# The index keys' projection of a two-layer trunk with x held in the array and 80 weight columns moving past it

## The chip, the cores and the metric

The kernel runs on one core of a Trainium2 chip, as one program. The metric is the device time in microseconds (us), the median of several runs. The profile is that of one execution of its own, whose time is given beside its span.

## What is computed

Two residual layers over 256 tokens of 2048 features, batch 1, all in float32. Layer 0 is a stick-breaking attention and an MLP; layer 1 is an indexer-selected sparse attention and an MLP (2048 to 8192, squared ReLU, back to 2048). The change lies in layer 1, in the indexer. Cut to what matters:

```python
h = rms_norm(x, norm_mix[1])
q, k, v, qi, ki, wi = split(h @ w_in_b)       # 2048, 512, 512, 1024, 64, 16 columns
qi = qi.reshape(b, s, 16, 64)
wi = wi * 16 ** -0.5
for each block of 128 queries:
    dots = einsum('bqhd,bkd->bqhk', qi_block, ki) * 64 ** -0.5
    score = einsum('bqh,bqhk->bqk', wi_block, relu(dots))
    sel = top_k(score where admissible, 64)
    ... softmax attention over the selected keys ...
```

`ki` is one index key of 64 features for each token, and `wi` one weight for each token and index head. Together they are 80 columns of `w_in_b`, and they are all that the change touches.

## The kernel before, in words

**Items.** All the dense work is one list of 738 items. An item is a block of weights, 128 partitions by 1024 numbers (two blocks of 128 rows by 512 columns). For each item the program loads the block from HBM by the SP queue (`load`, L815), splits it into a rounded part `wh` (a copy on ScalarE, L84) and the rest `wl` (a subtraction on VectorE, L839), and multiplies. Three matmuls stand for one product: x-high by w-high, x-high by w-low, x-low by w-high, all in the type fp32r. An ordinary item thus has 12 matmuls of 128 rows by 128 columns held in the array and 512 columns moving (L281 to L283). In these the activations `xT` (features on the partitions, tokens on the free side) are held and the weights move. Item i's multiplication stands in the program behind the split of item i+2 and the load of item i+7: five raw buffers, three split ones.

**The items of the indexer.** In the section of mixer B (`mixer_b`, L521), items 0 to 15 make the queries of the index heads (`qi`), items 16 and 17 the 80 columns of `ki` and `wi` (`ki_part`, L551), items 18 to 25 the attention's keys, and then queries, values and the output projection follow. `k0` is 18. The two items of `ki_part` are smaller blocks: 8 blocks of rows by 80 columns. They are the only dense items in which the weights are held (80 columns) and x moves: 16 matmuls with 512 columns moving, x-high and x-low side by side (L558), and 16 with 256 columns (L559).

**What follows the sums.** `ki_done` (L563) takes the sums, features first, out of PSUM: a copy on ScalarE (`kc`), an addition on VectorE (`ku`), a multiplication by `RS` into `kiT` (64 partitions), and a DMA on the ScalarE queue that copies it to partitions 64 to 127. `RS` holds each token's RMS scale along the free side; `row_scale_wide` (L231) makes it with two transposes on TensorE (L234) and a copy. `wi_step` (L574), two items later, turns the 16 columns of `wi` back to tokens first by two transposes on TensorE (L578).

**Turning by DRAM.** Other parts are turned by `to_features` (L156): VectorE transposes blocks of 32 by 32, four DMAs on the SP queue write the result to DRAM so many items later, and one DMA reads it back, turned, four items after that (`later`, L152, hangs a step on the end of an item).

**Order.** The scheduler may move an instruction within its engine; those passed through `keep` stand behind everything that the program gave that engine before. The steps of the indexer hang on items by hand (L783 to L789): `wi_step` at `k0+1`; eight score steps (L585, matmuls of 64 rows, a ReLU on ScalarE, four VectorE operations) at `k0+6` to `k0+12`; the causal limit at `k0+13`; top-k at `k0+14` to `k0+17`; the mask at `k0+18`. `acc` has three PSUM buffers of two banks, `aux` two of one bank, and the tile `jx`, which `to_features` fills, three buffers.

Of the kernel before, what the change touches and what calls it, by code (L numbers as in the profile page):

```python
# [9 lines left out]
F32 = mybir.dt.float32  # L10
# [7 lines left out]
P = 128  # L18
D = 2048
S = 256  # L20
KT = D // P
# [37 lines left out]
def trunk(ctx, tc, x, x_t, gains_t, w_in_a, w_out_a, w_in_b, w_out_b, rel_bias, w_up, w_down, out):  # L59


    nc = tc.nc
    x, out = x[0], out[0]
    w_in_a, w_out_a, w_in_b, w_out_b = w_in_a[0], w_out_a[0], w_in_b[0], w_out_b[0]

    consts = ctx.enter_context(tc.tile_pool(name="consts", bufs=1))
    wpool = ctx.enter_context(tc.tile_pool(name="wpool", bufs=3))
    tmp = ctx.enter_context(tc.tile_pool(name="tmp", bufs=2))
    accp = ctx.enter_context(tc.tile_pool(name="accp", bufs=3, space=PSUM))
    auxp = ctx.enter_context(tc.tile_pool(name="auxp", bufs=2, space=PSUM))  # L70
    drp = ctx.enter_context(tc.tile_pool(name="drp", bufs=1, space=bass.MemoryType.DRAM))

    act, dve, pool, pe = nc.scalar, nc.vector, nc.gpsimd, nc.tensor
# [5 lines left out]
    def pin(ins):  # L79
        if pinned[0]:  # L80
            keep(ins)

    def copy(o, i, scale=1.0):
        pin(act.activation(o, i, AF.Copy, scale=scale))  # L84
# [20 lines left out]
    ident = consts.tile([P, P], F32, name="ident")  # L105
# [19 lines left out]
    xT = consts.tile([P, KT, 2, S], F32R, name="xT")  # L125
    ss = consts.tile([P, 2, 4], F32, name="ss")
    rs = consts.tile([P, 2], F32, name="rs")
    consts.tile([P, 98], F32, name="pad2")
    RS = consts.tile([P, S], F32, name="RS")

    def load_x(lo, hi):
        pin(nc.sync.dma_start(xs[:, :, lo:hi], x[:, lo:hi].rearrange("(t p) d -> p t d", p=P)))
# [19 lines left out]
    def later(n, f, *a):  # L152

        due[clock[0] + n].append(lambda: f(*a))

    def to_features(parts, place, then, wait=0):  # L156


        n = sum(part.shape[1] // P for part in parts)
        y = tmp.tile([P, 8, P], F32, name="jx", bufs=3)[:, :n, :]  # L160
        m = 0
        for part in parts:
            k = part.shape[1] // P
            dve.transpose(y[:, m:m + k, :].rearrange("p k f -> p (k f)"), part)  # L164
            m += k
        d = drp.tile([4, 32, n, 4, 32], F32, name=f"td{n}", bufs=4)

        def write():
            for a in range(4):
                keep(nc.sync.dma_start(d[:, :, :, a, :].rearrange("b j n i -> j n b i"),  # L170
                                       y[32 * a:32 * a + 32].rearrange("p n (b i) -> p n b i", b=4)))
            later(4, read)

        def read():
            z = place()
            keep(nc.sync.dma_start(z, d.rearrange("b j n a i -> (b j) n (a i)")))
            if then is not None:
                later(4, then, z)

        later(1 + wait, write)  # L180
# [33 lines left out]
    def rsqrt(o, m, n):  # L214

        y = tmp.tile([P, 8], F32, name="rs_y")
        z = tmp.tile([P, 8], F32, name="rs_z")
        act.activation(y[:, :n], m, AF.Ln)
        act.activation(y[:, :n], y[:, :n], AF.Exp, scale=-0.5)
        dve.tensor_mul(z[:, :n], y[:, :n], y[:, :n])  # L220
        dve.tensor_mul(z[:, :n], z[:, :n], m)
        dve.tensor_scalar(z[:, :n], z[:, :n], -0.5, 1.5, op0=OP.mult, op1=OP.add)
        dve.tensor_mul(o, y[:, :n], z[:, :n])

    def row_scale():
        m = tmp.tile([P, 2], F32, name="rs_m")
        dve.tensor_reduce(m, ss, axis=AX.X, op=OP.add)
        dve.tensor_scalar(m, m, 1.0 / D, EPS, op0=OP.mult, op1=OP.add)
        rsqrt(rs, m, 2)

    def row_scale_wide():  # L231
        ps = auxp.tile([P, 512], F32, name="aux")
        for t in range(2):
            pe.transpose(ps[:, t * P:(t + 1) * P], rs[:, t:t + 1].to_broadcast([P, P]), ident)  # L234
        dve.tensor_copy(RS, ps[:, :S])


    accs = {}
# [1 line left out]
    def rows(w, r0, nr, c0, ncol):  # L240
        return w[r0:r0 + nr, c0:c0 + ncol].rearrange("(a p) c -> p a c", p=P)
# [279 lines left out]
    def mixer_b():  # L521
        items = []
        st = {}
# [17 lines left out]

        TOKS = (slice(0, P), slice(P, 384))

        def stats():
            row_scale()
            row_scale_wide()

        def qi_done(s, acc):
            to_features(acc, lambda: st["qiT"][:, s], None)

        def ki_part(q):  # L551
            def mm(wh, wl):
                if q == 0:
                    accs["ki"] = accp.tile([P, 2, 512], F32, name="acc")
                acc = accs["ki"]
                for j in range(8):
                    k = 8 * q + j
                    pe.matmul(acc[:80, 0, :], wh[:, j, :], xT[:, k, :, :], start=(k == 0), stop=False)  # L558
                    pe.matmul(acc[:80, 0, 0:S], wl[:, j, :], xT[:, k, 0, :], start=False,  # L559
                              stop=(k == KT - 1))  # L560
            return Item(rows(w_in_b, 8 * P * q, 8 * P, 4096, 80), 8, 80, mm)

        def ki_done():  # L563
            acc = accs.pop("ki")
            c = tmp.tile([P, S], F32, name="kc", bufs=1)
            u = tmp.tile([P, S], F32, name="ku", bufs=1)
            copy(c[:80, :], acc[:80, 0, S:])
            dve.tensor_add(u[:80, :], acc[:80, 0, :S], c[:80, :])
            kiT = st["kiT"]
            dve.tensor_mul(kiT[0:64, :], u[0:64, :], RS[0:64, :])  # L570
            nc.scalar.dma_start(kiT[64:128, :], kiT[0:64, :])
            st["u"] = u

        def wi_step():  # L574
            u = st.pop("u")
            ps = auxp.tile([P, 512], F32, name="aux")
            for t in range(2):
                pe.transpose(ps[:, t * P:t * P + 80], u[:80, t * P:(t + 1) * P], ident[:80, :80])  # L578
            r32 = tmp.tile([P, 2], F32, name="r32")
            dve.tensor_scalar_mul(r32, rs, HEADS ** -0.5 * IDX_D ** -0.5)  # L580
            for t in range(2):
                dve.tensor_scalar(st["wi"][:, t, :], ps[:, t * P + 64:t * P + 80], rs[:, t:t + 1],
                                  r32[:, t:t + 1], op0=OP.mult, op1=OP.mult)

        def score_step(m):  # L585

            kiT, sc = st["kiT"], st["sc"]
            halves = [slice(0, 64), slice(64, P)]
            ps = accp.tile([P, 2, 512], F32, name="acc")
            for t, cs, w in ((0, TOKS[0], P), (1, TOKS[1], S)):  # L590
                for i, lo in enumerate(halves):
                    keep(
                        pe.matmul(ps[:, i, cs], st["qiT"][lo, m // 4, 4 * t + m % 4], kiT[lo, 0:w],  # L593
                                  start=True, stop=True))
            rl = mk([P, 2, 384], "rl")
            act.activation(rl, ps[:, :, :384], AF.Relu)
            for i in range(2):
                h, r = 2 * m + i, rl[:, i, :]
                for t, cs in enumerate(TOKS):
                    w = st["wi"][:, t, h:h + 1]  # L600
                    if h == 0:
                        dve.tensor_scalar_mul(sc[:, cs], r[:, cs], w)
                    else:
                        dve.scalar_tensor_tensor(sc[:, cs], r[:, cs], w, sc[:, cs],
                                                 op0=OP.mult, op1=OP.add)
# [61 lines left out]
        def q_done(n, acc):  # L667
            r = normed(acc)
            if n < 3:
                to_features([r[:, t].rearrange("p h d -> p (h d)") for t in range(2)],  # L670
                            lambda: q_tile(n), None, 3)
            else:
                st["qn"] = r
# [88 lines left out]
        for s, q in side_by_side(2, QB):  # L762
            tokens_out(items, ("qi", s), w_in_b, 0, 3072 + 512 * s, lambda: xT, q,
                       lambda acc, s=s: qi_done(s, acc))
        items[10].post.append(stats)
        items += [ki_part(0), ki_part(1)]
        items[-1].post.append(ki_done)
        k0 = len(items)
        for q in range(QB):
            tokens_out(items, "k", w_in_b, 0, 2048, lambda: xT, q, k_done)  # L770
        for n in (0, 1, 2, "v", 3):
            for q in range(QB):
                if n == "v":
                    tokens_out(items, "v", w_in_b, 0, 2560, lambda: xT, q, v_done)
                else:
                    tokens_out(items, ("q", n), w_in_b, 0, 512 * n, lambda: xT, q,
                               lambda acc, n=n: q_done(n, acc))
        out_proj(items, w_out_b, lambda: st["oT"], 48, 3)

        def at(i, f, *a):  # L780
            items[i].post.append(lambda: f(*a))

        at(k0 + 1, wi_step)  # L783
        for m, d in enumerate((6, 6, 8, 8, 10, 10, 12, 12)):
            at(k0 + d, score_step, m)
        at(k0 + 13, admit)
        for r in range(TOPK // 8):
            at(k0 + 14 + r // 2, top_step)
        at(k0 + 18, mask_step)  # L789
        for n, j in enumerate((34, 42, 50, 58)):  # L790
            at(j, bias_load, n)
            at(j + 4, bias_mask, n, 0)
# [7 lines left out]


    sections = [mixer_a(), mlp(0, 16), mixer_b(), mlp(1, None)]
    items = [it for sec in sections for it in sec[0]]
    first = {}
    n = 0
# [96 lines left out]
```

## Time and profile before

| | us |
|---|---|
| median of 3 runs (2084.3 to 2085.76) | 2084.66 |
| time of the profiled execution | 2085.96 |
| its span, first to last instruction | 2084.2 |
| TensorE matmul busy | 2076.0 (100%) |
| TensorE weight loads busy | 1717.6 (82%) |
| VectorE busy | 1243.1 (60%) |
| ScalarE busy | 963.4 (46%) |

The mean granted TensorE clock was 0.999 of full speed. Busy time of matmuls is a union of records that overlap: a matmul's record lasts longer than the step to the next matmul, so what one costs is read from the starts of two that follow each other, not from its length. A group row gives the line, the engine, the operation, the tiles written and read, the shape, the count, then busy us, the mean length of one in ns, and the idle time before it with what ended it. PE is TensorE's matmuls, PEld its weight loads, DVE is VectorE, ACT ScalarE, POOL GpSimd, SPq and ACTq the DMA issues of two queues. In a shape such as 128\*80, 128 rows and 80 columns are held.

### The profile page before, as it was taken

The page shows a single profiled execution, that of the slowest core. Times are in us where ns is not written, and L with a number is a line of the kernel's source. Part 1 is how long each engine was busy: PE and PEld are TensorE (multiplying, and loading weights), DVE is VectorE, ACT ScalarE, POOL GpSimd, SP SyncE. Part 2 cuts the span into 40 slices and gives each one's busy share as a digit, 9 for nine tenths or more (in the row PEclk, how much of TensorE's full clock was granted, in tenths as well). Part 3 has the DMA queues.
Part 4 walks back from the last instruction along what each step waited for, and adds up shares of the span by engine and source line. Part 5 has one row for each costly group of instructions (what it writes and reads, how often), then busy time and mean ns, then how long its engine had stood idle before and what let it go on. Part 6 is the DMA issues. An engine that isn't in the chain of part 4 may idle for free.

```text
span 2084.2 us, 24647 instructions
## 1 busy us (share of the span) xinstructions
PE 2076.0 (100%) x9256; PEld 1717.6 (82%) x9256; DVE 1243.1 (60%) x1350; ACT 963.4 (46%) x1164; POOL 25.8 (1%) x71
## 2 busy tenths in 40 slices
PE   9999999999999999999999999999999999999999
PEld 7888888888888888888888788888888888888887
DVE  5646655666655565565565898666565555555554
ACT  6545554544443443443454566554444344344433
POOL 0200000000000000000000000000000000000000
PEclk9999999999999999999999999999999999999999
DMA  8788857888866876886788698498887687688664
GB/s 294 221 239 218 238 172 200 260 243 247 231 214 196 242 223 196 233 233 192 214 254 245 183 256 255 142 274 232 258 234 213 193 235 231 194 226 244 192 203 150
DMA packets 477448, 464.83 MB, mean 223 GB/s; under 512 B 269648, under 2 KB 279952, under 8 KB 477328
## 3 DMA queue, kind: packets, MB, share of 16 engines
q1 hardware_dynamic: 469472, 455.81, 75.3%
q10 hardware_dynamic: 7856, 7.45, 1.4%
q8 instruction: 72, 1.18, 0.2%
q14 instruction: 48, 0.39, 0.1%
HBM read 425.90 MB, written 37.22 MB: 222 GB/s over the span
## 4 chain that ended last, share of the span: by engine, by line
PE 99%; DMA 0%; ACT 0%; DVE 0%; SPq 0%; issue 0%; DVEq 0%
PE acc L281 31%; PE acc L283 31%; PE acc L282 31%; PE acc L254 1%; PE aux L705 1%; PE acc L415 0%; PE aux L461 0%; DMA wraw<-in_w_in_a_dram 0%; PE acc L593 0%; PE aux L282 0%; PE aux L283 0%; PE aux L281 0%; PE acc L558 0%; PE acc L417 0%; PE aux L462 0%; PE aux L755 0%
## 5 line engine op out<-in xcount | busy, mean ns | idle before, releaser
L839 DVE TENSOR_TENSOR w<-wraw,w 128x1024 fp32r<-128x1024 f32 (+1 forms) x739 | 901.0, 1220 | 759.8 <-ACT w L84 755.6
L84 ACT ACTIVATE w<-wraw 128x1024 fp32r<-128x1024 f32 (+1 forms) x739 | 784.2, 1061 | 1037.2 <-PE acc L283 983.9
L282 PE MATMUL acc<-w,xT 128*128 128x512 f32 x1632 | 638.3, 391 | 0.0
L281 PE MATMUL acc<-w,xT 128*128 128x512 f32 x1632 | 637.4, 391 | 0.0
L283 PE MATMUL acc<-w,xT 128*128 128x512 f32 x1632 | 636.8, 390 | 0.0
L281 PE MATMUL acc<-w,hT 128*128 128x512 f32 x992 | 386.4, 389 | 0.0
L282 PE MATMUL acc<-w,hT 128*128 128x512 f32 x992 | 386.4, 389 | 0.0
L283 PE MATMUL acc<-w,hT 128*128 128x512 f32 x992 | 386.3, 389 | 0.0
L283 PEld LDWEIGHTS acc<-w,xT 128*128 128x128 f32 x1632 | 306.6, 188 | 63.9 <-issue 0.7
L281 PEld LDWEIGHTS acc<-w,xT 128*128 128x128 f32 x1632 | 306.7, 188 | 63.7 <-ACT w L84 0.3
L282 PEld LDWEIGHTS acc<-w,xT 128*128 128x128 f32 x1632 | 306.7, 188 | 63.5 <-issue 0.7
L282 PEld LDWEIGHTS acc<-w,hT 128*128 128x128 f32 x992 | 186.3, 188 | 38.6
L283 PEld LDWEIGHTS acc<-w,hT 128*128 128x128 f32 x992 | 186.3, 188 | 38.5
L281 PEld LDWEIGHTS acc<-w,hT 128*128 128x128 f32 x992 | 186.3, 188 | 38.5
L281 PE MATMUL acc<-w,oT 128*128 128x512 f32 x256 | 100.4, 394 | 0.0
L282 PE MATMUL acc<-w,oT 128*128 128x512 f32 x256 | 99.6, 390 | 0.0
L283 PE MATMUL acc<-w,oT 128*128 128x512 f32 x256 | 99.1, 391 | 0.0
L281 PEld LDWEIGHTS acc<-w,oT 128*128 128x128 f32 x256 | 48.1, 188 | 10.1 <-ACT junk L643 0.4
L283 PEld LDWEIGHTS acc<-w,oT 128*128 128x128 f32 x256 | 48.1, 188 | 9.9
L282 PEld LDWEIGHTS acc<-w,oT 128*128 128x128 f32 x256 | 48.1, 188 | 9.8
L164 DVE STREAM_TRANSPOSE jx<-acc 128x512 f32<-128x512 f32 x68 | 44.7, 695 | 14.4 <-PE acc L283 10.8
L297 DVE SCALAR_TENSOR_TENSOR xs<-acc,rs,xs 128x512 f32<-128x512 f32 x56 | 39.5, 746 | 11.2 <-PE acc L283 11.2
(149 smaller groups left out, 789.0 us busy)
## 6 DMA issues: line engine op xcount, KB each, us to landing
wraw<-in_w_up_dram SPq DMA_DIRECT2D x256, 512.0 KB, 4.1
wraw<-in_w_down_dram SPq DMA_DIRECT2D x256, 512.0 KB, 4.8
wraw<-in_w_in_a_dram SPq DMA_DIRECT2D x95, 512.0 KB, 4.8
wraw<-in_w_in_b_dram SPq DMA_DIRECT2D x64, 512.0 KB, 4.7
td<-jx SPq DMA_DIRECT2D x240, 128.0 KB, 4.5
jx<-td SPq DMA_DIRECT2D x45, 512.0 KB, 6.2
wraw<-in_w_out_a_dram SPq DMA_DIRECT2D x32, 512.0 KB, 4.0
wraw<-in_w_out_b_dram SPq DMA_DIRECT2D x32, 512.0 KB, 4.6
```

The lines of the kernel that those rows point to most:

```text
L84: pin(act.activation(o, i, AF.Copy, scale=scale))
L164: dve.transpose(y[:, m:m + k, :].rearrange("p k f -> p (k f)"), part)
L254: pin(pe.matmul(accs[key][t], L[:, j, part, t * P:(t + 1) * P], wx[:, j, :], start=(j == 0 and n == 0), stop=False))
L281: pin(pe.matmul(acc[t], L[:, k, 0, ts], wh[:, j, :], start=(k == 0), stop=False))
L282: pin(pe.matmul(acc[t], L[:, k, 0, ts], wl[:, j, :], start=False, stop=False))
L283: pin(pe.matmul(acc[t], L[:, k, 1, ts], wh[:, j, :], start=False, stop=(k == KT - 1)))
L297: dve.scalar_tensor_tensor(xc, acc[t], scale[:, t:t + 1], xc, op0=OP.mult, op1=OP.add)
L705: pe.matmul(ps[:, h - lo, :], qT[:, GRP * t + h, :], kT[:, n, 0:w], start=True, stop=True)
L839: pin(dve.tensor_sub(wl[:, a], raw[:, a], wh[:, a].bitcast(F32)))
```

## The change

The 80 columns are now what moves, and x is held, as in the ordinary items. For each half of the tokens and each of 16 blocks of features there are three matmuls with 128 by 128 of x held and 80 columns moving; the sums come out with tokens on the partitions. There each token's scale is one number for its partition, so `RS`, `row_scale_wide` and `wi_step` go: two ScalarE copies scale `ki` and write it twice side by side (`u`), and VectorE scales `wi` straight from PSUM. `ki` is then turned by `to_features`: one VectorE transpose of 256 columns, four writes to DRAM at item 18, one read at item 22 that fills all 128 partitions of `kiT`; the DMA on the ScalarE queue goes. The score steps, the causal limit, top-k and the mask hang one item later. The split parts of these two items begin 8 numbers further into their buffer, as in the ordinary items (`moving`). The tiles `RS` and `kc` (1 KB for each partition) are no longer allocated.

```diff
-    RS = consts.tile([P, S], F32, name="RS")
...
-        def stats():
-            row_scale()
-            row_scale_wide()
+        stats = row_scale
...
-                for j in range(8):
-                    k = 8 * q + j
-                    pe.matmul(acc[:80, 0, :], wh[:, j, :], xT[:, k, :, :], start=(k == 0), stop=False)
-                    pe.matmul(acc[:80, 0, 0:S], wl[:, j, :], xT[:, k, 0, :], start=False,
-                              stop=(k == KT - 1))
-            return Item(rows(w_in_b, 8 * P * q, 8 * P, 4096, 80), 8, 80, mm)
+                for t in range(2):
+                    ts = slice(t * P, (t + 1) * P)
+                    for j in range(8):
+                        k = 8 * q + j
+                        for n, (i, w) in enumerate(((0, wh), (0, wl), (1, wh))):
+                            pe.matmul(acc[:, t, :80], xT[:, k, i, ts], w[:, j, :],
+                                      start=(k, n) == (0, 0), stop=(k, n) == (KT - 1, 2))
+            return Item(rows(w_in_b, 8 * P * q, 8 * P, 4096, 80), 8, 80, mm, True)
...
-            c = tmp.tile([P, S], F32, name="kc", bufs=1)
-            u = tmp.tile([P, S], F32, name="ku", bufs=1)
-            copy(c[:80, :], acc[:80, 0, S:])
-            dve.tensor_add(u[:80, :], acc[:80, 0, :S], c[:80, :])
-            kiT = st["kiT"]
-            dve.tensor_mul(kiT[0:64, :], u[0:64, :], RS[0:64, :])
-            nc.scalar.dma_start(kiT[64:128, :], kiT[0:64, :])
-            st["u"] = u
-
-        def wi_step():
-            u = st.pop("u")
-            ps = auxp.tile([P, 512], F32, name="aux")
-            for t in range(2):
-                pe.transpose(ps[:, t * P:t * P + 80], u[:80, t * P:(t + 1) * P], ident[:80, :80])
+            u = tmp.tile([P, 2, 2, 64], F32, name="ku", bufs=1)
             r32 = tmp.tile([P, 2], F32, name="r32")
             dve.tensor_scalar_mul(r32, rs, HEADS ** -0.5 * IDX_D ** -0.5)
             for t in range(2):
-                dve.tensor_scalar(st["wi"][:, t, :], ps[:, t * P + 64:t * P + 80], rs[:, t:t + 1],
+                copy(u[:, t], acc[:, t, :64].unsqueeze(1).to_broadcast([P, 2, 64]),
+                     scale=rs[:, t:t + 1])
+                dve.tensor_scalar(st["wi"][:, t, :], acc[:, t, 64:80], rs[:, t:t + 1],
                                   r32[:, t:t + 1], op0=OP.mult, op1=OP.mult)
+            to_features([u.rearrange("p t i f -> p (t i f)")],
+                        lambda: st["kiT"].rearrange("p (t q) -> p t q", t=2), None)
...
-        at(k0 + 1, wi_step)
-        for m, d in enumerate((6, 6, 8, 8, 10, 10, 12, 12)):
+        for m, d in enumerate((7, 7, 9, 9, 11, 11, 13, 13)):
             at(k0 + d, score_step, m)
-        at(k0 + 13, admit)
+        at(k0 + 14, admit)
         for r in range(TOPK // 8):
-            at(k0 + 14 + r // 2, top_step)
-        at(k0 + 18, mask_step)
+            at(k0 + 15 + r // 2, top_step)
+        at(k0 + 19, mask_step)
```

## Rows read from the trace of the kernel before

**Rows 1.** the page, part 1 (busy us, share of the span, instructions) and the start of part 4

```profile
PE 2076.0 (100%) x9256; PEld 1717.6 (82%) x9256; DVE 1243.1 (60%) x1350; ACT 963.4 (46%) x1164; POOL 25.8 (1%) x71
...
PE 99%; DMA 0%; ACT 0%; DVE 0%; SPq 0%; issue 0%; DVEq 0%
```

**Rows 2.** the waits of TensorE: us in total, times, longest

```profile
PE acc L254 <- ACT w L84: 2.0, 2, 1.7
```

**Rows 3.** groups of TensorE by shape: count, busy us, mean ns of one, idle before

```profile
L281 PE MATMUL acc<-w,xT 128*128 128x512 f32 x1632 | 637.4, 391 | 0.0
...
L558 PE MATMUL acc<-xT,w 128*80 128x512 f32 x16 | 5.6, 395 | 0.0
...
L559 PE MATMUL acc<-xT,w 128*80 128x256 f32 x16 | 4.5, 280 | 0.0
...
L578 PE MATMUL aux<-ident,ku 80*128 80x80 f32 x2 | 0.3, 232 | 0.0
```

**Rows 4.** TensorE in order of time over the index's two items: start, length (us)

```profile
1127.39 0.39 PE L283 MATMUL acc<-w,xT 128*128 128x512 f32 x1
1127.62 0.40 PE L558 MATMUL acc<-xT,w 128*80 128x512 f32 x1
1127.86 0.28 PE L559 MATMUL acc<-xT,w 128*80 128x256 f32 x1
1127.97 0.40 PE L558 MATMUL acc<-xT,w 128*80 128x512 f32 x1
...
1133.23 0.40 PE L281 MATMUL acc<-w,xT 128*128 128x512 f32 x1
```

**Rows 5.** TensorE around the two transposes of rs

```profile
1100.17 0.39 PE L281 MATMUL acc<-w,xT 128*128 128x512 f32 x1
1100.40 0.38 PE L234 MATMUL aux<-ident,rs 128*128 128x128 f32 x2
...
1100.85 0.39 PE L283 MATMUL acc<-w,xT 128*128 128x512 f32 x1
```

**Rows 6.** TensorE around the two transposes of ku

```profile
1138.49 0.40 PE L283 MATMUL acc<-w,xT 128*128 128x512 f32 x1
1138.72 0.30 PE L578 MATMUL aux<-ident,ku 80*128 80x80 f32 x2
...
1139.14 0.39 PE L282 MATMUL acc<-w,xT 128*128 128x512 f32 x1
```

**Rows 7.** weight loads (PEld) behind the transposes of ku: start, length

```profile
1138.80 0.19 PEld L281 LDWEIGHTS acc<-w,xT 128*128 128x128 f32 x1
1138.91 0.19 PEld L282 LDWEIGHTS acc<-w,xT 128*128 128x128 f32 x1
```

**Rows 8.** weight loads behind the first two score steps

```profile
1154.14 0.19 PEld L281 LDWEIGHTS acc<-w,xT 128*128 128x128 f32 x1 [0.33 <-ACT w L84]
1154.25 0.19 PEld L282 LDWEIGHTS acc<-w,xT 128*128 128x128 f32 x1
```

**Rows 9.** ScalarE behind the index's sums: start, length, count

```profile
1133.43 0.38 ACT L84 ACTIVATE kc<-acc 80x256 f32<-80x256 f32 x1 [1.74 <-PE acc L559]
```

**Rows 10.** groups of VectorE behind the index's sums, by shape

```profile
L568 DVE TENSOR_TENSOR ku<-acc,kc 80x256 f32<-80x256 f32 x1 | 0.4, 421 | 0.9 <-ACT kc L84 0.9
L570 DVE TENSOR_TENSOR kiT<-ku,RS 64x256 f32<-64x256 f32 x1 | 0.4, 418 | 0.0
```

**Rows 11.** the SP queue: four writes of the heads' index, start, length, count

```profile
1132.31 4.48 SPq L170 DMA_DIRECT2D td<-jx  x4
```

**Rows 12.** DMA issues of 1125 to 1165 us: KB of one, median us to landing

```profile
wraw<-in_w_in_b_dram SPq DMA_DIRECT2D x13, 512.0 KB, 4.6
...
w<-td SPq DMA_DIRECT2D x2, 512.0 KB, 6.9
```

**Rows 13.** busy us of PE, PEld, DVE, ACT, POOL by stretch; clock, DMA share, GB/s

```profile
1133.00:1152.00 19.00, 19.00 (x87) 15.63 (x86) 9.57 (x11) 7.72 (x8) 0.00 (x0) 1.00 0.98 294
...
1185.00:1200.00 15.00, 15.00 (x68) 12.44 (x67) 15.00 (x51) 9.91 (x24) 0.00 (x0) 1.00 0.72 212
```

More of the change, by code (lines that the diff above doesn't have):

```diff
@@ L229, in row_scale @@
         rsqrt(rs, m, 2)
-    def row_scale_wide():
-        ps = auxp.tile([P, 512], F32, name="aux")
-        for t in range(2):
-            pe.transpose(ps[:, t * P:(t + 1) * P], rs[:, t:t + 1].to_broadcast([P, P]), ident)
-        dve.tensor_copy(RS, ps[:, :S])
     accs = {}
@@ L555, in mm @@
                 acc = accs["ki"]
-                for j in range(8):
-                    k = 8 * q + j
-                    pe.matmul(acc[:80, 0, :], wh[:, j, :], xT[:, k, :, :], start=(k == 0), stop=False)
-                    pe.matmul(acc[:80, 0, 0:S], wl[:, j, :], xT[:, k, 0, :], start=False,
-                              stop=(k == KT - 1))
-            return Item(rows(w_in_b, 8 * P * q, 8 * P, 4096, 80), 8, 80, mm)
+                for t in range(2):
[6 more added lines that the diff above has]
+            return Item(rows(w_in_b, 8 * P * q, 8 * P, 4096, 80), 8, 80, mm, True)
         def ki_done():
             acc = accs.pop("ki")
-            c = tmp.tile([P, S], F32, name="kc", bufs=1)
-            u = tmp.tile([P, S], F32, name="ku", bufs=1)
-            copy(c[:80, :], acc[:80, 0, S:])
-            dve.tensor_add(u[:80, :], acc[:80, 0, :S], c[:80, :])
-            kiT = st["kiT"]
-            dve.tensor_mul(kiT[0:64, :], u[0:64, :], RS[0:64, :])
-            nc.scalar.dma_start(kiT[64:128, :], kiT[0:64, :])
-            st["u"] = u
-        def wi_step():
-            u = st.pop("u")
-            ps = auxp.tile([P, 512], F32, name="aux")
-            for t in range(2):
-                pe.transpose(ps[:, t * P:t * P + 80], u[:80, t * P:(t + 1) * P], ident[:80, :80])
+            u = tmp.tile([P, 2, 2, 64], F32, name="ku", bufs=1)
             r32 = tmp.tile([P, 2], F32, name="r32")
```

## The prediction

> **What bounds the kernel now.** I read the page's busy times and its chain first. TensorE's matmuls are busy for 2076.0 of 2084.2 us, and the chain that ended last is TensorE for 99% [rows 1]. The waits of TensorE come next, to see whether that busy time hides stalls: the largest group is 2.0 us in two waits, at line 254, which is not in the code of this change [rows 2]. So TensorE goes from one matmul to the next almost without a gap, and what counts is the step from one start to the next. Third are the groups by shape, for the counts; their mean lengths of 391, 395 and 280 ns overlap and are no price [rows 3]. Prices come from the orders of time: an ordinary matmul with 512 columns moving steps by 0.23 us, one with 256 columns by 0.11 us [rows 4]. An item of 12 thus takes 2.7 us. The other engines work ahead of TensorE, so their work costs time only where it makes a split, a PSUM buffer or `kiT` late.
>
> **The change, part by part, on TensorE.**
>
> The old multiplication goes. Its 32 matmuls run from 1127.62 to 1133.23 us, where the next item's first matmul starts: 5.61 us [rows 4].
>
> The two transposes of `rs` go. With them, 0.68 us lie between the ordinary matmuls at 1100.17 and 1100.85, with one ordinary matmul between; two ordinary steps are 0.46 us. That gives 0.22 us [rows 5]. The two transposes of `ku` go: from 1138.49 to 1139.14 are 0.65 us against 0.46 again, so 0.19 us [rows 6]. Together 6.02 us are removed.
>
> The new multiplication has 2 halves of the tokens by 16 blocks of features by 3 matmuls: 96, against 32 before. Each holds 128 columns of x and moves 80. No row shows that shape, so it is bounded. From below, the moving columns alone: 256 take 0.11 us, so 80 in proportion would take 0.034 us, 3.3 us in all, and the change would give back 2.7 us. From above, the whole record of a weight load, 0.19 us [rows 7], with nothing overlapped: 18.2 us, a loss of 12.2 us. Between these lies what a load costs when the matmul in front of it is too short to cover it. Two places show that. Behind the short transposes of `ku` (two matmuls of 232 ns within 0.30 us, so 0.07 us apart [rows 3, 6]) the load at 1138.80 is followed by the next one at 1138.91 [rows 7]. Behind the score steps, after TensorE's loads had stood idle for 0.33 us, the loads start at 1154.14 and 1154.25 [rows 8]. Both are 0.11 us, in both the load was of 128 by 128 of `xT`, and in neither was there moving work of 0.11 us to wait for. So I take 0.11 us for each of the 96: the load sets the step, and the 80 columns run in its shadow. A held operand used twice running saves nothing: lines 281 and 282 hold the same x, and each matmul still has a load of its own, 9256 loads for 9256 matmuls [rows 1]. That makes 10.56 us. The read-off error of two decimals is a few ns a matmul: 0.105 to 0.118 us make 10.1 to 11.3 us.
>
> Sum on TensorE: 10.56 less 6.02 is **+4.5 us** (4.1 to 5.3 by that reading).
>
> **The change on the other engines.** ScalarE loses one copy of 0.38 us [rows 9] and a DMA issue and gets two copies of about that size; the next split waits behind them by some 0.4 us, and splits are made two items, 5.4 us, ahead: nothing. VectorE loses 0.42 and 0.42 us behind the sums [rows 10] and the copy to `RS`, and gets one transpose of 256 columns; it is busy for 9.57 of the 19 us there [rows 13]: nothing. If that cover were gone, either would cost at most its own length, under 0.5 us.
>
> The SP queue gets four writes and a read. The writes wait for the turn of VectorE, and behind them stand the loads of weights. Four writes of the heads' index held SP for 4.48 us [rows 11], with four times the bytes of these, so 4.48 us bounds them from above. A load is issued five items, 13.6 us, before its split and lands in 4.6 us [rows 12]: 9.0 us are spare, so nothing. The two items themselves grow by 4.5 us and need no more bytes, which helps the loads.
>
> `kiT` now comes by DRAM. Its read is due at the end of item 22 and the first score at the end of item 25: three items, 8.2 us. The two larger reads at this place took 6.9 us to land [rows 12]. I take nothing; TensorE would stand still for each us over 8.2.
>
> The score steps, the causal limit, top-k and the mask issue the same instructions one item later. Nothing is added, but VectorE has room from 1133 to 1152 us and none from 1185 to 1200, where it is busy for 15.00 of 15.00 us [rows 13]. One item's worth of room is given up ahead of a full stretch. The splits are in that same queue. The cost lies between nothing and that one item, 2.7 us; less than nothing has no cause, since no wait of TensorE at these steps is there to be saved [rows 2]. I take nothing, because TensorE had no wait in that full stretch before, and keep the end for the range. The memory that `RS` and `kc` leave moves other tiles; I take nothing, since 1632 matmuls that read three weight buffers at different places show one mean [rows 3].
>
> The profiled execution took 2085.96 us, 1.8 us over its span and 1.3 us over the median of the runs. Its own sum is 2085.96 + 4.5 = 2090.5 us; against the median 2084.66 it is **2089.2 us**, or +0.22%.
>
> **The rivals.**
>
> *Quick loads (not slower).* Place: the 96 new loads. If short matmuls let loads follow at the 0.07 us that the two `ku` transposes show [rows 6], the new multiplication takes 6.7 us and the change +0.7 us: 2085.4 us. The point from which it decides is 0.106 us a matmul, where the loss falls to 0.2%; at 0.063 us it would be nothing. For it: those two matmuls had loads as well. Against it: they are transposes, and the two loads of `xT` in a like place were 0.11 us apart [rows 7, 8]. The Trainium skill, "TensorE: Matmul & The Clock Gate", section "Back-to-back issue gap", speaks for a value between: it gives about 81 ns for a pair of weight load and matmul with 128 columns moving in a sustained stream. By that the 96 would take 7.8 us, an estimate, and the kernel 2086.4 us; the 0.11 us of the rows is not what it says. Chance 0.12.
>
> *VectorE falls behind.* The indexer's steps, one item later, run into the full stretch, a split comes late, and TensorE waits for 1 to 2.7 us between items 26 and 45: 2090.2 to 2091.9 us. For it: VectorE at 100% there [rows 13]. Against it: the scheduler can put splits ahead of top-k. Chance 0.18.
>
> *`kiT` is late.* The read through DRAM lands after 8.2 us, with DMA engines 98% busy in the stretch before [rows 13]; two us late makes 2091.2 us. Against it: a quarter of the bytes, and three items of time. Chance 0.05.
>
> *Nothing overlaps.* Load and matmul run one after the other at 0.19 us: 2096.8 us. Against it: the two pairs of loads 0.11 us apart. Chance 0.05.
>
> The forecast itself keeps 0.60.
>
> **How the numbers follow.** A difference of 0.2%, 4.2 us, is about what a measurement of this kernel can tell from no change. The forecast lies 0.3 us over it, and the runs of before spread over 1.5 us, so of its 0.60 I put 0.37 over the bound and 0.23 within. Slower: 0.37 + 0.18 + 0.05 + 0.05 = 0.65. Within: 0.23, and quick loads with most of their 0.12, 0.33. Faster, 0.02, is what is left of quick loads near the lower bound. The range takes the forecast with its reading error, the late splits and the late `kiT`: 2087.0 to 2092.0 us. It leaves out quick loads and the serial case, 0.17.
>
> **What would show it.** In the profile after, the 96 matmuls of `ki_part` start 0.11 us apart and the two items take 10.6 us where they took 5.61; steps of 0.07 or 0.04 us would prove the pricing wrong. Lines 234 and 578 are gone. TensorE's waits stay as small as in [rows 2]; a new wait of a score matmul for a DMA, or of an ordinary matmul for VectorE's split near the top-k steps, would be the second or third rival. TensorE's busy time should rise by the same 4 to 5 us as the span.

## The result and the profile after

The changed kernel takes 2099.36 us (median of 6 runs, 2098.23 to 2101.81) against 2084.61 us: 14.75 us slower, ratio 1.007 [1.0059, 1.0081]. I had forecast 2089.2 us and a range that ended at 2092.0. Its profiled execution took 2098.23 us with a span of 2096.5 us; it is the quickest of the six, so its profile shows rather less than the whole loss: the two profiled spans lie 12.3 us apart (2084.2 and 2096.5).

The page's part 1 and the start of part 4, which answer to [rows 1]:

```profile
PE 2086.8 (100%) x9316; PEld 1727.3 (82%) x9316; DVE 1241.8 (59%) x1348; ACT 963.3 (46%) x1165; POOL 25.9 (1%) x71
...
PE 96%; DVE 2%; DMA 1%; ACT 1%; issue 0%; SPq 0%; DVEq 0%; ACTq 0%
```

TensorE is still the bound, with 60 matmuls more: 64 in the index, and the four transposes gone. But the chain now has some work of VectorE, the DMAs and ScalarE in it.

Lines are numbered anew in this kernel: the ordinary matmuls, L281 to L283 before, are L274 to L276 here. The 96 new matmuls in order of time, first whole and then in two stretches, where equal neighbours are merged (start, length of the whole, count):

```profile
1125.62 15.13 PE L553 MATMUL acc<-w,xT 128*128 128x80 f32 x96
...
1126.76 2.52 PE L553 MATMUL acc<-w,xT 128*128 128x80 f32 x21
...
1132.66 5.75 PE L553 MATMUL acc<-w,xT 128*128 128x80 f32 x26
```

One record lasts 0.28 us in the first stretch and 0.41 us in the second, so the steps are (2.52 - 0.28) / 20 = 0.112 us and (5.75 - 0.41) / 25 = 0.214 us. The first is the step that the prediction had. The second is twice as long. The busy time by stretch shows why (PE, PEld, DVE, ACT, POOL busy with counts; then the granted clock, DMA share, GB/s):

```profile
1126.00:1131.00 5.00, 5.00 (x47) 5.00 (x47) 2.24 (x3) 0.88 (x1) 0.00 (x0) 1.00 1.08 207
...
1131.50:1132.00 0.50, 0.50 (x5) 0.50 (x5) 0.00 (x0) 0.50 (x1) 0.00 (x0) 0.54 0.62 102
...
1132.00:1140.00 8.00, 8.00 (x40) 8.00 (x39) 1.23 (x1) 0.16 (x1) 0.00 (x0) 0.50 0.84 189
1141.00:1145.00 4.00, 4.00 (x11) 3.03 (x11) 2.07 (x4) 1.37 (x3) 0.00 (x0) 0.50 0.13 18
1146.00:1150.00 4.00, 4.00 (x19) 3.30 (x18) 1.58 (x2) 1.91 (x2) 0.00 (x0) 1.00 0.46 95
```

The granted clock is full in the first stretch and half (1.2 of 2.4 GHz) in those of 1132 and 1141; it fell between 1131.5 and 1132, some 5.9 us into the run, though TensorE's matmuls and weight loads are recorded as busy without a gap. It is still at half when the ordinary matmuls resume:

```profile
1139.91 0.84 PE L553 MATMUL acc<-w,xT 128*128 128x80 f32 x3
1140.55 0.77 PE L274 MATMUL acc<-w,xT 128*128 128x512 f32 x1
1141.13 0.63 PE L275 MATMUL acc<-w,xT 128*128 128x512 f32 x1
...
1144.97 0.51 PE L275 MATMUL acc<-w,xT 128*128 128x512 f32 x1
1145.31 0.39 PE L276 MATMUL acc<-w,xT 128*128 128x512 f32 x1
1145.54 0.40 PE L274 MATMUL acc<-w,xT 128*128 128x512 f32 x1
```

Those with 512 columns moving step by 0.43 us, and 0.23 us again only from 1145.31. In [rows 4] the same two items took 5.61 us; here the 96 begin at 1125.62 and the next item at 1140.55, 14.9 us.

Last, the waits of TensorE inside the section, two that [rows 2] had no counterpart for (total, times, longest):

```profile
PE acc L274 <- ACT junk L629: 1.3, 1, 1.3
...
PE acc L274 <- ACT rl L582: 0.3, 1, 0.3
```

Both are ordinary matmuls that wait for a PSUM buffer `acc` until ScalarE has read it, behind the norm's squares (`junk`) and behind a score step's ReLU (`rl`).

### The profile page after: what moved, and what is told of

Same layout as the page of the kernel before. It is cut to its first block, busy times and chain, and to the rows that moved or that the text cites. A ratio compares the mean times of both kernels' runs of the same rounds, so it can differ in the third digit from the quotient of the medians.

```text
span 2096.5 us, 24767 instructions
## 1 busy us (share of the span) xinstructions
PE 2086.8 (100%) x9316; PEld 1727.3 (82%) x9316; DVE 1241.8 (59%) x1348; ACT 963.3 (46%) x1165; POOL 25.9 (1%) x71
## 4 chain that ended last, share of the span: by engine, by line
PE 96%; DVE 2%; DMA 1%; ACT 1%; issue 0%; SPq 0%; DVEq 0%; ACTq 0%
PE acc L274 30%; PE acc L275 30%; PE acc L276 30%; PE acc L247 1%; PE acc L553 1%; DVE w L824 1%; PE aux L691 0%; PE acc L408 0%; PE aux L454 0%; PE aux L276 0%; PE aux L275 0%; PE aux L274 0%; DMA wraw<-in_w_in_a_dram 0%; DMA qTb<-td 0%; ACT w L84 0%
## 5 line engine op out<-in xcount | busy, mean ns | idle before, releaser
L274 PE MATMUL acc<-w,xT 128*128 128x512 f32 x1632 | 637.6, 391 | 0.3 <-ACT rl L582 0.3
L276 PE MATMUL acc<-w,xT 128*128 128x512 f32 x1632 | 636.7, 390 | 0.0
L274 PE MATMUL acc<-w,hT 128*128 128x512 f32 x992 | 385.9, 389 | 0.0
L276 PE MATMUL acc<-w,hT 128*128 128x512 f32 x992 | 385.9, 389 | 0.0
L274 PEld LDWEIGHTS acc<-w,xT 128*128 128x128 f32 x1632 | 307.0, 188 | 64.9 <-issue 1.0
L276 PEld LDWEIGHTS acc<-w,xT 128*128 128x128 f32 x1632 | 307.0, 188 | 64.3 <-issue 0.3
L276 PEld LDWEIGHTS acc<-w,hT 128*128 128x128 f32 x992 | 186.2, 188 | 38.6
L274 PEld LDWEIGHTS acc<-w,hT 128*128 128x128 f32 x992 | 186.2, 188 | 38.6
L274 PE MATMUL acc<-w,oT 128*128 128x512 f32 x256 | 100.3, 394 | 1.3 <-ACT junk L629 1.3
L276 PE MATMUL acc<-w,oT 128*128 128x512 f32 x256 | 99.0, 391 | 0.0
L274 PEld LDWEIGHTS acc<-w,oT 128*128 128x128 f32 x256 | 48.1, 188 | 11.5 <-ACT junk L629 1.7
L276 PEld LDWEIGHTS acc<-w,oT 128*128 128x128 f32 x256 | 48.1, 188 | 9.9
L163 DVE STREAM_TRANSPOSE jx<-acc 128x512 f32<-128x512 f32 x68 | 44.7, 695 | 14.4 <-PE acc L276 10.8
```

The lines of the kernel that those rows point to most:

```text
L274: pin(pe.matmul(acc[t], L[:, k, 0, ts], wh[:, j, :], start=(k == 0), stop=False))
L276: pin(pe.matmul(acc[t], L[:, k, 1, ts], wh[:, j, :], start=False, stop=(k == KT - 1)))
```

## The experiments

Theory after this reading: the loss has three parts. Weight loads set the step (as forecast, some 5 us). The long run of matmuls that move little takes the clock to half (some 6.5 us). The later place of the score and top-k steps makes waits (some 3 us). The rival was that the steps behind the sums, with their way through DRAM, hold most of the loss, and that the clock's fall is of little weight or belongs to the place. Each group of runs had its own runs of the kernel before on the same chip: medians 2084.84 us for the first two groups, 2084.74 for the last. The changed kernel was not run again with them; its 2099.36 us is compared across, where the kernel before differs by 0.2 us.

**Four short runs in place of a long one.** The 96 matmuls are issued as four items of 24, each behind four ordinary items. (Not shown: everything behind hangs two items later in the list.)

```diff
-        items += [ki_part(0), ki_part(1)]
+            if n % 4 == 3:
+                items.append(ki_part(n // 4))
```

> The 96 matmuls are issued as four items of 24, each behind four ordinary items, in place of one run of 96; the later steps hang two items later in the list. Clock theory (the long run of matmuls with 80 columns moving takes the granted clock to half, and that costs some 6.5 us): the clock stays full, the 96 still step by 0.11 us, so about 2084.6 + 5.1 - 0.4 for the matmuls and some 2.7 for the waits behind, 2092 us (2090 to 2094). Rival (the clock's fall costs little, the loss is in the steps behind the sums): 2097 to 2100 us, as the changed kernel.

Measured: 2093.84 us, ratio 1.0043 [1.0028, 1.0058]. In order of time, one of the four:

```profile
1106.39 0.39 PE L276 MATMUL acc<-w,xT 128*128 128x512 f32 x1
1106.62 2.77 PE L553 MATMUL acc<-w,xT 128*128 128x80 f32 x24
1109.22 0.48 PE L274 MATMUL acc<-w,xT 128*128 128x512 f32 x1
```

24 take 2.60 us, the clock does not fall at any of the four, and the matmuls behind them are at full pace. So the same 96 matmuls without the long fall save 5.5 us, in a kernel that is otherwise not quite the same. It also has waits of its own further on, because all that hangs behind it moved: the keys' index comes 1.0 us late from DRAM here, and a PSUM buffer 2.0 us late.

```profile
PE acc L274 <- ACT junk L629: 2.0, 1, 2.0
...
PE acc L579 <- DMA kiT<-td: 1.0, 1, 1.0
```

Behind the wait of 2.0 us the clock did fall, for some 3 us of ordinary matmuls that step by 0.43 us:

```profile
1295.51 0.50 PE L274 MATMUL acc<-w,oT 128*128 128x512 f32 x1 [1.99 <-ACT junk L629]
...
1296.00:1299.00 3.00, 3.00 (x9) 2.33 (x8) 2.53 (x4) 2.93 (x5) 0.00 (x0) 0.50 0.08 14
```

This was the slowest of four executions, 2096.21 us; the two whose mean granted clock is given as 1.0 took 2092.00 and 2092.42 us. In this execution the wait was thus followed by a loss of clock on top of its own length.

**Fewer matmuls, wider.** x-high meets w-high and w-low in one matmul.

```diff
-                        for n, (i, w) in enumerate(((0, wh), (0, wl), (1, wh))):
-                            pe.matmul(acc[:, t, :80], xT[:, k, i, ts], w[:, j, :],
-                                      start=(k, n) == (0, 0), stop=(k, n) == (KT - 1, 2))
+                        pe.matmul(acc[:, t, :160].rearrange("p (h c) -> p h c", h=2),
+                                  xT[:, k, 0, ts], it.both[:, :, j, :], start=k == 0, stop=False)
+                        pe.matmul(acc[:, t, :80], xT[:, k, 1, ts], wh[:, j, :],
+                                  start=False, stop=k == KT - 1)
```

> x-high meets w-high and w-low in one matmul with 160 columns moving, x-low a matmul with 80: 64 matmuls in place of 96, and a copy and an addition join the two sums. If the weight load sets the step, 64 x 0.112 = 7.2 us at full clock. Clock theory does not say whether this mix keeps the clock: if it does, 2084.6 - 6.0 + 7.2 + 2.7 = 2088.5 us; if it falls some 4.4 us into the run, 2.8 us are doubled and the ordinary matmuls behind lose 2.1 us, 2093 us. If the columns set the step, the 160-column matmuls would take more than the 80-column ones.

Measured: 2088.55 us, ratio 1.0019 [1.0009, 1.0029]. In order of time, and the stretch of the 64:

```profile
1125.74 0.32 PE L552 MATMUL acc<-w,xT 128*128 128x160 f32 x1
1125.90 0.24 PE L554 MATMUL acc<-w,xT 128*128 128x80 f32 x1
1125.96 0.32 PE L552 MATMUL acc<-w,xT 128*128 128x160 f32 x1
1126.12 0.24 PE L554 MATMUL acc<-w,xT 128*128 128x80 f32 x1
```

```profile
1125.00:1132.00 7.00, 7.00 (x66) 7.00 (x64) 3.65 (x4) 2.12 (x2) 0.00 (x0) 1.00 0.94 168
```

A pair takes 0.22 us, two loads of 0.11, so a third of the loads less is a third of the time less. With this mix the clock stays full. The 4.4 us that the expectation of this run and that of the 32 matmuls give for the fall are a misreading: in the profile after it came 5.9 us into the run.

**The later place alone.** The kernel before, with only the numbers of the hanging steps changed.

```diff
-        for m, d in enumerate((6, 6, 8, 8, 10, 10, 12, 12)):
+        for m, d in enumerate((7, 7, 9, 9, 11, 11, 13, 13)):
...
-        at(k0 + 18, mask_step)
+        at(k0 + 19, mask_step)
```

> The kernel before with one part of the change alone: score steps, causal limit, top-k and mask hang one item later. If the 2.7 us that the changed kernel loses behind the index come from these later steps, 2087.3 us (2086.3 to 2088.3). If they come from the way through DRAM or the ScalarE copies, 2084.6 us within 0.5.

Measured: 2088.11 us, ratio 1.0014 [1.0004, 1.0023], 3.3 us more with no matmul changed. The two profiles, which both have a stretch at half clock in the first 20 us, differ by 2.3 us in span (2086.5 and 2084.2). Its groups of TensorE have the two waits of the changed kernel, in the idle time at the end of the rows:

```profile
L281 PE MATMUL acc<-w,xT 128*128 128x512 f32 x1632 | 636.7, 390 | 0.3 <-ACT rl L596 0.3
...
L281 PE MATMUL acc<-w,oT 128*128 128x512 f32 x256 | 100.3, 394 | 1.0 <-ACT junk L643 1.0
```

**A third of the matmuls.** One matmul for each half of the tokens and block of features in place of three; the two products with the rests are left out, so `ki` and `wi` are less exact.

```diff
-                        for n, (i, w) in enumerate(((0, wh), (0, wl), (1, wh))):
-                            pe.matmul(acc[:, t, :80], xT[:, k, i, ts], w[:, j, :],
-                                      start=(k, n) == (0, 0), stop=(k, n) == (KT - 1, 2))
+                        pe.matmul(acc[:, t, :80], xT[:, k, 0, ts], wh[:, j, :],
+                                  start=k == 0, stop=k == KT - 1)
```

> Leaves out the two cross products of ki and wi (x-high by w-low, x-low by w-high): 32 matmuls in place of 96, 3.6 us, shorter than the 4.4 us after which the clock fell. Clock theory: the clock stays full, 2084.6 - 6.0 + 3.6 + 2.7 = 2084.9 us (2083.5 to 2086). Rival (the loss is behind the sums): 2092 us or more, since only 64 matmuls of 0.11 us are saved on 2099.4.

Measured: 2085.44 us, ratio 1.0003 [0.9994, 1.0012]. The stretch of the 32 is at full clock:

```profile
1126.00:1129.50 3.50, 3.50 (x33) 3.46 (x32) 2.87 (x4) 2.12 (x2) 0.00 (x0) 1.00 0.87 200
```

Leaving out 64 of 96 matmuls saves 13.9 us, twice what 64 steps of 0.112 us are worth; the rest, 6.7 us, is of the size of the clock's part. One of the ten executions took 2088.54 us at a mean granted clock of 0.998; no trace of it was kept, so whether the run of 32 brought the clock down in it stays open.

**Three times the columns.** One run of 96 again, but each block of 80 columns is moved three times over in its matmul.

```diff
-                            pe.matmul(acc[:, t, :80], xT[:, k, i, ts], w[:, j, :],
+                            pe.matmul(acc[:, t, :240].rearrange("p (r c) -> p r c", r=3),
+                                      xT[:, k, i, ts],
+                                      w[:, j, :].unsqueeze(1).to_broadcast([P, 3, 80]),
```

> The changed kernel with each block of 80 columns moved three times over in the same matmul (240 columns moving, into 240 columns of PSUM, of which the first 80 are used): still one run of 96 matmuls with as many weight loads. Theory (the clock falls because too little moves in each step, not because of the number of loads or of short steps): a step stays near 0.112 us, the clock stays full, and the time is 2084.8 + 5.3 - 0.4 + 3 = 2092.7 us (2091 to 2094), though three times as much moves. Rival (weight loads back to back, or matmuls in quick succession, bring the clock down): the clock falls as before, 2098 to 2102 us.

Measured: 2092.44 us, ratio 1.0034 [1.0021, 1.0047]: 6.9 us less than the changed kernel, for three times the moving work. In order of time, and the stretch:

```profile
1125.98 10.94 PE L553 MATMUL acc<-w,xT 128*128 128x240 f32 x96
1136.76 0.40 PE L274 MATMUL acc<-w,xT 128*128 128x512 f32 x1
```

```profile
1126.00:1136.70 10.70, 10.70 (x97) 10.70 (x96) 3.65 (x4) 2.13 (x2) 0.00 (x0) 1.00 1.04 196
```

96 matmuls take 10.78 us, still 0.112 us each, and the clock is full throughout. The number of loads and the step are those of the changed kernel at full clock; what differs is the columns that move in each step, and with them the columns written in PSUM. So neither the loads back to back nor the quick succession of matmuls brings the clock down by itself: with 80 columns moving it fell, with 240 it did not.

**The place undone.** The changed kernel with the hanging steps back at the items of before.

```diff
-        for m, d in enumerate((7, 7, 9, 9, 11, 11, 13, 13)):
+        for m, d in enumerate((6, 6, 8, 8, 10, 10, 12, 12)):
...
-        at(k0 + 19, mask_step)
+        at(k0 + 18, mask_step)
```

> The changed kernel with score steps, causal limit, top-k and mask back at the items of the kernel before. If the later place alone costs the 3.3 us that the kernel before lost with it, 2099.4 - 3 = 2096.4 us (2095 to 2098), and no score matmul waits for the DMA, since the turned keys landed 4 us ahead of the first score. If the way through DRAM needs that item, TensorE waits for the DMA and the time stays at 2098 to 2101 us.

Measured: 2096.69 us, ratio 1.0057 [1.0042, 1.0072], 2.7 us less than the changed kernel. No score matmul waits for the DMA: the new way through DRAM did not need the item that it was given. In the profiled execution one attention matmul does wait for another turn, 1.9 us. That execution is the slowest of the four (2099.59 us; the others 2095.45 to 2097.02), so its wait and its clock are not those of the median:

```profile
PE aux L691 <- DMA qTb<-td: 1.9, 1, 1.9
...
1126.60:1129.90 3.30, 3.30 (x32) 3.30 (x30) 2.42 (x3) 1.06 (x1) 0.00 (x0) 1.00 0.87 196
1130.00:1143.00 13.00, 13.00 (x63) 13.00 (x63) 1.23 (x1) 1.06 (x1) 0.00 (x0) 0.50 0.75 153
```

The run of 96 begins at 1126.55 here, and the clock falls some 3.3 us into it, against 5.9 us in the profile after. How soon it falls, and so what it costs, is thus not the same each time; over the six executions of the changed kernel, too, the mean granted clock goes from 0.995 to 0.997.

**Both mended.** The wide form with the steps at the items of before; its edits are those of the second experiment and the one above.

> The 64 matmuls with 160 and 80 columns moving, and the later steps at the items of the kernel before. Load-bound theory: 64 x 0.112 = 7.1 us in place of 6.0, the clock full, nothing late: 2084.8 + 1.1 = 2085.9 us (2085 to 2087.5). If the later place was not what cost 3 us, 2088.5 us as with the steps one item later.

Measured: 2085.71 us, ratio 1.0004 [0.9995, 1.0014]: no difference to the kernel before that can be measured. Against the wide form with the later steps, 2088.55 us, the place is worth 2.8 us, a third measure of it. Here too no score matmul waits for the DMA, with the run of matmuls at full clock.

**The run elsewhere.** The kernel before with a run of the same shape in the first MLP, far from the indexer.

```diff
+        def extra():
+            ps = auxp.tile([P, 512], F32, name="aux")
+            for n in range(96):
+                keep(pe.matmul(ps[:, :80], xT[:, n % 16, n // 48, 0:P], tri[:, :80],
+                               start=True, stop=True))
...
+        if l == 0:
+            items[48].post.append(extra)
```

> The kernel before with 96 matmuls of the same shape added in the middle of the first MLP, where nobody uses their result: x held, 80 columns of a constant moving. Clock theory: 96 x 0.112 = 10.7 us, and the clock falls in the run and takes some 6.5 us more: 2084.8 + 17.2 = 2102 us (2099.5 to 2104.5). If the fall belongs to the indexer's place (what stands around it, the DMAs there), the clock stays full and the time is 2095.5 us.

Measured: 2102.96 us, ratio 1.0087 [1.007, 1.0104], 18.1 us for 96 matmuls. The run, and the time by stretch:

```profile
519.21 14.98 PE L376 MATMUL aux<-tri,xT 128*128 128x80 f32 x96
...
519.30:525.00 5.70, 5.70 (x54) 5.70 (x52) 2.17 (x2) 2.01 (x2) 0.00 (x0) 1.00 0.92 188
525.30:526.00 0.70, 0.70 (x6) 0.70 (x5) 0.00 (x0) 0.00 (x0) 0.00 (x0) 0.50 0.89 155
526.00:533.00 7.00, 7.00 (x35) 7.00 (x34) 0.00 (x0) 0.00 (x0) 0.00 (x0) 0.50 0.17 58
534.00:538.50 4.50, 4.50 (x12) 3.53 (x13) 0.00 (x0) 0.00 (x0) 0.00 (x0) 0.50 0.00 0
540.00:545.00 5.00, 5.00 (x23) 4.14 (x23) 3.59 (x3) 1.72 (x3) 0.00 (x0) 1.00 0.34 103
```

The clock goes to half in the run and stays there into the ordinary matmuls, as at the index. Here it fell 6.1 us into the run, which began at 519.21. VectorE, ScalarE and the DMAs stand nearly still from 526 to 538.5 us, so the clock stays at half without work of theirs beside it; and no indexer is near.

**Earlier still.** The kernel before with the hanging steps one item earlier, to see whether their place has more to give.

```diff
-        for m, d in enumerate((6, 6, 8, 8, 10, 10, 12, 12)):
+        for m, d in enumerate((5, 5, 7, 7, 9, 9, 11, 11)):
...
-        at(k0 + 18, mask_step)
+        at(k0 + 17, mask_step)
```

> The kernel before with score steps, causal limit, top-k and mask hung one item earlier. One item later cost 3.3 us through waits of TensorE for PSUM buffers. In the kernel before TensorE has no such wait, so theory: nothing to gain, 2084.8 us within 1. Rival (each item of place is worth some 3 us, early as late): 2081.5 us, which would beat both kernels.

Measured: 2085.13 us, ratio 1.0002 [0.9993, 1.0011]. Nothing. Its profile too has a wait of 0.3 us behind a score step's ReLU. None of the versions beats the kernel before.

## Why the prediction was wrong

The sign was right and the size was off by three. By its own steps:

- *The work removed, 6.02 us.* It is gone: neither the old multiplication nor the four transposes have rows after.
- *"So I take 0.11 us for each of the 96."* Right at full clock: 0.112 us in the profile after, and 10.78 us for the 96 when nothing disturbs them. The quick loads' 0.07 us and the serial 0.19 us did not occur as a sustained step. The Trainium skill, "TensorE: Matmul & The Clock Gate", section "LDWEIGHTS (loading the stationary operand)", gives the columns held divided by 1.2 as a load's time in ns, by which 128 columns would take 107 ns, an estimate. The 112 ns measured at full clock are 5 ns above it. The 81 ns that the prediction quoted from the same page's section "Back-to-back issue gap" for a sustained pair were not seen with these operands.
- *"Sum on TensorE: 10.56 less 6.02 is +4.5 us."* **Here it failed.** The sum multiplied 96 by a price read at full clock and nowhere asked whether the clock would stay full through 96 matmuls whose columns, by its own lower bound, need 0.034 of each 0.11 us. It fell to half. In the profile some 42 steps of the run cost 0.214 in place of 0.112 us, 4.3 us, and 11 ordinary steps (1140.55 to 1145.31, 4.76 us in place of 2.5) another 2.3 us: 6.6 us together. The run with three times the columns, which keeps the step of 0.112 us and the full clock, puts it at 2099.36 - 2092.44 = 6.9 us; the waits for PSUM buffers in its profile are nearly those of the changed kernel (1.6 and 0.3 us against 1.3 and 0.3). I read [rows 1] as a TensorE that can only be busy, and took busy for full speed; the clock did not enter even as a rival.
- *The later score and top-k steps: "I take nothing, because TensorE had no wait in that full stretch before."* Wrong by 3 us. That TensorE had no wait there was no evidence for a moved schedule. The kernel before with that one edit loses 3.3 us, the changed kernel without it gains 2.7, and the wide form without it 2.8. The rival "VectorE falls behind" came near the size, 1 to 2.7 us, but by luck. Its mechanism did not show: the waits that these two profiles name are for PSUM buffers that ScalarE has not read yet, not for a split, and the longer one stands at 1299.9 us in the changed kernel, at the output projection and far behind the top-k steps. They make 1.3 to 1.6 us of the 3; where the rest stands was not separated, nor why ScalarE reads later.
- *`kiT` by DRAM in time.* Right, and with more room than I had thought. The rows of its tile in the changed kernel (the read's issue, the first score matmuls, the landing time):

```profile
L579 PE MATMUL acc<-kiT,w x64: 269/374/378, 1164.7 to 1190.0; 64*128 64x128 f32 x32, 64*128 64x256 f32 x32
L175 SPq DMA_DIRECT2D kiT<-td x1: 418/418/418, 1156.8 to 1156.8; - x1
...
DMA to landing us min/median/max: 4.0/4.0/4.0
```

  It landed at 1160.8, 3.9 us ahead of the first score.
- *ScalarE, VectorE, the SP queue: nothing.* The wide form, which has all of them and one copy and one addition more, is within 0.9 us of the kernel before once the place is undone, and its longer multiplication alone accounts for 64 x 0.112 - 6.0 = 1.2 us; so they cost nothing that can be told apart.

The parts against the runs: loads 96 x 0.112 - 6.0 = 4.8 us, clock 6.9 us, place 2.7 to 3.3 us, together 14.4 to 15.0; measured 14.75. The clock's part is itself a difference to the changed kernel, so what agrees is the rest: loads and place, 7.5 to 8.1 us, against the 7.6 us by which the run with three times the columns is behind the kernel before.

## What to carry to other kernels

Before holding the big operand and moving the small one, count the loads: a matmul with 128 columns held stepped by 0.112 us here whether 80 or 240 columns moved, so the room between 80 and 240 was time that nobody used. A long run with few columns moving also took TensorE's clock down, and then it is paid twice, in the run and in the good matmuls behind it. Both remedies that were tried kept the clock full there: breaking the run up, and giving each matmul more columns. And a step that is hung one item later, "to be safe", is an edit with a price of its own: price it by the buffers that its neighbours then hold longer, and try it alone.

## What the runs showed of the hardware

- The granted clock fell to half while matmuls and weight loads were both recorded busy for 100% of the stretch. The Trainium skill, "TensorE: Matmul & The Clock Gate", section "Why this matters for your kernels", advises to keep TensorE busy and free of long idle gaps, to avoid drops of throughput. Here no gap is recorded, and that was not enough.
- 96 matmuls of 128 held and 80 moving columns in one run brought it down, at two places of the program; 96 with 240 moving, 64 with 160 and 80 in turn, one run of 32 with 80, and runs of 24 with 80 between ordinary items did not, each in the one execution that was profiled. The fall came 5.9, 6.1 and 3.3 us into the run in three traces; the run of 32 lasts about 3.5 us. What in the columns counts for the clock was not separated.
- At half clock the load's pace halves as well: 0.214 us a step against 0.112. In both places over 4 us of ordinary matmuls ran at half clock (1140.55 to 1144.97, and 534 to 538.5) before it was full again. A half-clock stretch of some 3 us also followed a wait of 2.0 us (at 1295.51 in the four short runs).
- 240 columns moved in the 0.112 us that 80 took, and 160 with 80 took two such steps in turn, 0.16 and 0.06 us: the pair, not the single start, is what two loads set.
